# A trunk kernel's MLP: another order of the seven products, two additions fewer, and an eighth PSUM bank

## The chip, the core and the metric

The kernel runs on one core of one Trainium2 chip. The metric is the device time of one execution in microseconds (us); the time before is the median of three runs. Engines are named as in the profile: PE is TensorE, PEld its weight loads, DVE VectorE, ACT ScalarE, POOL GpSimd, SP SyncE.

## The reference, cut to what matters

One layer on a sequence of 512 rows of 1024 channels, in fp32: a token-mixing sub-layer (window attention, spatial gating, pooling, gates), cross-attention into 256 memory rows, and a squared-ReLU MLP, each between RMSNorms. The change touches the MLP, and the PSUM banks of everything before it:

```
hf = rmsnorm(x, g_norm[l, 4])
yf = jnp.square(jax.nn.relu(hf @ w_up[l])) @ w_down[l]     # w_up 1024 x 4096, w_down 4096 x 1024
x = x + rmsnorm(yf, g_norm[l, 5])
```

## The kernel before

Every fp32 factor is split into a high and a low part in the type fp32r (`split`: ACT casts the high part, DVE subtracts it from the source), and each product is three matmuls (`mm3`): high by high, high by low, low by high. PE's instructions keep their program order; the other engines' order is set by the tile framework's scheduler when the program is built. Each engine, and each DMA queue, works its own instructions in order.

The 4096 hidden rows come in 32 blocks of 128. Blocks 0 to 7 are made by plain products (`up`, step `U`). Blocks 8 to 31 are made two at a time (`two`, step `V`) by a scheme with seven half-sized products in place of eight (60 matmuls of 256 columns in the step, 24 left over for the next). The blocks are then used in four groups (`FIRST`, `NPAIR`: 4, 8, 8, 8 blocks) and a rest of four that a plain product takes at the end (`down`, step `D`). The product of a group with w_down is again done with seven products (`product`, step `M g i`, i from 1 to 7), two row tiles `tb` each. A product leaves its sum in PSUM bank y or z of its `tb`, and `ADDED` says into which quarter of the result (`acc`, tiles `c`) DVE adds that bank, and with which sign. Products 7, 6 and 4 accumulate onto the bank that product 1 began, 3 onto the one that 5 began.

The two last products of a step `V` are held back (`rest`): product 7 of the pair (`seventh`) runs between the two row tiles of the next step `M`, product 4 (`fourth`) after them. Both use one bank; DVE's `add(c22, c22, y)` has to read it between them.

The order of the steps is written out by hand. The operands of a step are prepared two steps ahead (`prepare`, called at the end of each step): `ready` splits the group's blocks (tiles `wloa`), forms sums of them (tiles `s`), and splits w_down's tiles (`wlob` from `q`). Products 1, 5, 6 and 4 all use one set of weight tiles, `qs[g, (0, 0)]`: after each of the first three has been split, `plus` adds the next quarter of w_down onto it by an accumulating DMA on POOL's queue, as the next of these products needs. `two_ready` loads and splits w_up's tiles (`wraw` into `wlou`). Their buffers, four `wraw`, are shared with the quarters (1, 0) and (1, 1) of w_down for products 2 and 3, and their DMAs stand in SP's queue in program order.

Before the MLP, PSUM has a pool of seven banks that `bank()` hands out in turn, and one bank, `t0`, that lies idle until the MLP.

Of the kernel before, what the change touches and what calls it, by code (L numbers as in the profile page):

```python
# [10 lines left out]
F32 = mybir.dt.float32  # L11
# [5 lines left out]
P = 128  # L17
# [5 lines left out]
M = 256  # L23
# [39 lines left out]
def trunk(ctx: ExitStack, tc: tile.TileContext, xT, xt0, memT, wst, cst, vec, rows, wsp, wpl, out):  # L63
# [8 lines left out]
    p1 = ctx.enter_context(tc.tile_pool(name="p1", bufs=1, space=bass.MemoryType.PSUM))  # L72
    cp = ctx.enter_context(ExitStack())
    pp = cp.enter_context(tc.tile_pool(name="pp", bufs=7, space=bass.MemoryType.PSUM))
# [7 lines left out]
    def slot(name, dt=F32, shape=None):  # L82
        return sl.tile(shape or [P, S], dt, name=name, tag="slot", bufs=NSLOT)
# [12 lines left out]
    def pair_of(pool, name):  # L96
        return tuple(pool.tile([P, S], F32R, name=name + z, tag="act", bufs=2 * KD) for z in "hl")

    def bank(name="ps"):
        return pp.tile([P, 512], F32, name=name, tag="ps")  # L100


    keep = tc.keep_in_program_order
# [46 lines left out]
    def split(hi, lo, src, order=free):  # L150
        return (order(nc.scalar.copy(hi, src)).ins,  # L151
                order(nc.vector.tensor_tensor(lo, src, hi.bitcast(F32), op=ALU.subtract)).ins)  # L152

    def split_scaled(hi, lo, src, g, order=free):
        order(nc.scalar.activation(hi, src, AF.Identity, scale=g))
        order(nc.vector.scalar_tensor_tensor(lo, src, g, hi.bitcast(F32), op0=ALU.mult, op1=ALU.subtract))
# [10 lines left out]
    def cut(act, lo, hi):  # L167
        return tuple(z[:, lo:hi] for z in act)

    def halfcut(hf):  # L170
        return hf * HALF, (hf + 1) * HALF
# [41 lines left out]
    with ExitStack() as c1:  # L213
# [9 lines left out]


        warm, ps = slot("warm"), bank()
        nc.vector.memset(warm[:, :P], 0.0)
        nc.vector.memset(ones, 1.0)
# [68 lines left out]
        def quad(name, dt=F32R):  # L296
            return a.tile([P, 4, S], dt, name=name, tag="y", bufs=4)
# [98 lines left out]
        c, u = quad("c", F32), quad("u", F32)  # L396
# [62 lines left out]
        def sub(o, p, q):  # L459
            nc.vector.tensor_tensor(o, p, q, op=ALU.subtract)  # L460

        def add(o, p, q):
            nc.vector.tensor_tensor(o, p, q, op=ALU.add)  # L463
# [4 lines left out]
        def each(y):  # L468
            return [tuple(z[:, b, :] for z in y) for b in range(4)]
# [9 lines left out]
        def quarters(j):  # L479

            lo, hi = rows2[j], rows2[2 + j]
            with tc.issue_after(exps[-1]):
                for i in range(2):
                    for r, k in ((lo, 2 * j + i), (hi, 4 + 2 * j + i)):
                        nc.scalar.activation(r[:, i, :], r[:, i, :], AF.Identity, scale=vc[:, V_G + k:V_G + k + 1])
            a0, a1, b0, b1 = lo[:, :, :HALF], lo[:, :, HALF:], hi[:, :, :HALF], hi[:, :, HALF:]

            def cast(i, src, sign=None):
                h, l = (z[:, 2 * j:2 * j + 2, :] for z in xs[i])
                if sign:  # L490
                    split_scaled(h, l, src, sign)
                else:
                    split(h, l, src)

            sub(b1, b1, a1)
            cast(5, b1)
            sub(a1, a0, a1)
            cast(7, a1)
            add(a0, a0, b1)
            cast(6, a0, -1.0)  # L500
            sub(b0, a0, b0)
            cast(3, b0)
# [132 lines left out]
        def merged(hf):  # L635
# [18 lines left out]
        steps = [("B", 0, 0), ("B", 0, 1), ("S",), ("P",)] + [("G", 0, i) for i in G] + [("G", 1, i) for i in G] + [  # L654
            ("B", 1, 0), ("B", 1, 1)] + [("G", 2, i) for i in G] + [("E", 0), ("E", 1)]
# [293 lines left out]
    with ExitStack() as c3:  # L949
        f = c3.enter_context(tc.tile_pool(name="f", bufs=1))  # L950
# [26 lines left out]
        def tiles_of(g, ab):  # L977

            n = NPAIR[g] // 2
            at = T_DN + FIRST[g] + (2 * ab[0] + ab[1]) * n  # L980
            return range(at, at + n)
# [20 lines left out]
        for j in range(UPK, UP0):  # L1002
            ps = bank()
# [7 lines left out]
        def held(name):  # L1011
            return pools.get(name, pools.get("")).tile([P, 512], F32, name=name, tag=name)

        for j in range(UP0):
            ps = held("t0") if j == UP0 - 1 else bank()
# [27 lines left out]
        def quarters():  # L1043

            def joined(hf, c, t):
                for j in range(4):
                    h, l = cut(xf[4 * c + j], *halfcut(hf))
                    add(t[:, j, :], h.bitcast(F32), l.bitcast(F32))
                return t

            def room(name, tag, bufs):
                return f.tile([P, 4, HALF], F32, name=name, tag=tag, bufs=bufs)

            def new(i):
                h, l = (f.tile([P, 4, HALF], F32R, name=f"xs{i}{z}", tag="xs", bufs=6) for z in "hl")
                xs[i] = [(h[:, j, :], l[:, j, :]) for j in range(4)]
                return h, l

            a21, a22 = joined(1, 0, room("x21", "s", 2)), joined(1, 1, room("x22", "q", 4))
            sub(a22, a22, a21)  # L1060
            a11 = joined(0, 0, room("x11", "q", 4))
            sub(a21, a11, a21)
            split(*new(7), a21)
            add(a11, a11, a22)
            split_scaled(*new(6), a11, -1.0)
            for j in range(4):
                for part in cut(xf[4 + j], *halfcut(0)):
                    sub(a11[:, j, :], a11[:, j, :], part.bitcast(F32))
            split(*new(3), a11)

            def last():
                for j in range(4):
                    split(*xs[5][j], a22[:, j, :])

            return last
# [75 lines left out]
        acc, sums = {}, {}  # L1151
# [16 lines left out]
        def ready(g, i):  # L1168

            def new(name):  # L1170
                t = f.tile([P, 4, HALF], F32, name=name, tag="s", bufs=2)
                sums[g, name] = [t[:, j:j + 2, :] for j in range(0, NPAIR[g], 2)]
                return sums[g, name]

            def each(op, *of):
                for z in zip(*of):
                    op(*z)

            def plus(ab, of):

                for q, i in zip(qs[g, ab], tiles_of(g, of)):
                    nc.gpsimd.dma_start(q, wst[i], accum_op=ALU.add)  # L1182

            a0, a1 = halves(g, 0)
            if i == 1:
                first, second = a0, (0, 0)
            if i == 7:
                first, second = new("s3"), (0, 1)
                each(sub, first, a0, a1)
            if i > 1 and i != 7:  # L1190
                b0, b1 = halves(g, 1)
            if i == 5:
                first, second = new("s1"), (0, 0)
                each(sub, first, b1, a1)
            if i == 6:
                first, second = sums[g, "s1"], (0, 0)
            if i == 4:
                first, second = b1, (0, 0)
            if i == 3:
                first, second = sums[g, "s1"], (1, 1)  # L1200
                each(sub, first, first, b0)
            if i == 2:
                first, second = b0, (1, 0)
            if i in (2, 3):
                loads(g, second)
            act, ws = parts(g, first, i), []
            if i == 5:
                each(add, first, first, a0)
            for q in qs[g, second]:
                w = parts_of(f"b{i}")  # L1210
                split(*w, q)
                ws.append(w)
            if i in (1, 5, 6):
                plus((0, 0), {1: (0, 1), 5: (1, 1), 6: (1, 0)}[i])
            return act, ws
# [1 line left out]


        BANKS = {1: "y", 7: "y", 6: "y", 4: "y", 5: "z", 3: "z", 2: "y"}
        ADDED = {1: ((0, 0, 1), (0, 1, -1)), 7: ((0, 1, 1),), 6: ((0, 1, -1), (1, 1, -1)), 4: ((1, 0, 1),),  # L1220
                 5: ((1, 1, -1),), 3: ((0, 1, -1),), 2: ((0, 0, 1),)}
        banks = {}

        def product(g, i, act, ws, between=None):
            for tb in range(2):
# [5 lines left out]
                for j in range(NPAIR[g]):  # L1231
# [3 lines left out]
                    for n, (q1, q2) in enumerate(((0, 0), (0, 1), (1, 0))):  # L1235
                        mm(ps, lhsT=w1[q1], rhs=w2[q2], start=new and j == 0 and n == 0,
                           stop=j == NPAIR[g] - 1 and n == 2, skip_group_check=not new)
                for hf, c, sign in ADDED[i]:
                    if (hf, c, tb) not in acc:
# [58 lines left out]
            return finish  # L1298


        steps = [("M", 0, 1), ("U", 5), ("M", 0, 5), ("U", 6), ("M", 0, 7), ("M", 0, 6), ("U", 7), ("M", 0, 3), ("M", 0, 4), ("M", 0, 2)]
        for g in range(1, 4):
            u = FIRST[g] + 4
            steps += [("V", u), ("M", g, 1), ("V", u + 2), ("M", g, 7), ("V", u + 4), ("M", g, 5), ("M", g, 6), ("V", u + 6),
                      ("M", g, 4), ("M", g, 3), ("M", g, 2)]
        steps += [("D",)]

        def prepare(st):
# [24 lines left out]
        for n, st in enumerate(steps):  # L1333
# [6 lines left out]
            elif st[0] == "M":  # L1340
                product(st[1], st[2], *got.pop(n), rest)
                if rest and steps[n - 1][1] >= FIRST[4]:
                    for j in range(2):
                        i = steps[n - 1][1] + j
# [85 lines left out]
```

## Time and profile before

| | |
|---|---|
| median of three runs | 794.5 us (792.24 to 796.3) |
| the profiled execution: time, span | 793.82 us, 792.1 us |
| PE busy | 777.4 us, 98% of the span |
| DVE, ACT, POOL busy | 616.0, 472.1, 65.6 us |
| granted clock of PE | 0.998 of full speed |

The times of the profile count from the span's start; the profiled execution is 1.7 us longer than its span. The MLP's first group begins near 484 us, the three equal groups run from 522 to 762 us, and `down` ends the kernel.

### The profile page before, as it was taken

Reading aid. Unit: us, or ns where it says so; the run is one execution under the profiler, and the core shown is the slowest. Engines: PE = TensorE matmul, PEld = TensorE weight load, DVE = VectorE, ACT = ScalarE, POOL = GpSimd, SP = SyncE. Lnnn points to the kernel's source line nnn. Section 1 sums busy time; section 2 is a strip of 40 time slices with the busy share of each in tenths; the row PEclk is TensorE's granted clock in tenths of the full one; section 3 lists DMA queues with packets and bytes.
Section 4 is the critical chain, followed back from the end, with each engine's and each line's share of the span. In section 5 each row is a group of like instructions: output and inputs, shape, how many; then the busy total and the mean of one; then the engine's idle time right before and its main releaser. Section 6 shows DMA issues by size and latency. Waiting matters only on the chain.

```text
span 792.1 us, 11400 instructions
## 1 busy us (share of the span) xinstructions
PE 777.4 (98%) x4250; PEld 670.6 (85%) x4250; DVE 616.0 (78%) x942; ACT 472.1 (60%) x877; POOL 65.6 (8%) x93
## 2 busy tenths in 40 slices
PE   9999999999999999999999999999999999999996
PEld 7887778878888888888888899899899989888985
DVE  6677975888758656568758759898899877998966
ACT  7327879756563463544757576667565755565732
POOL 0000000200101000251100010010100010001000
PEclk9999999999999999999999999999999999999999
DMA  6443222735756233653322454584676357546522
GB/s 231 160 141 126 80 80 64 202 78 188 167 207 138 75 107 107 228 212 122 109 102 66 173 161 107 173 217 142 115 224 167 134 107 211 155 152 122 164 81 101
DMA packets 34567, 112.79 MB, mean 142 GB/s; under 512 B 4176, under 2 KB 4688, under 8 KB 34512
## 3 DMA queue, kind: packets, MB, share of 16 engines
q1 hardware_dynamic: 27296, 86.64, 32.0%
q0 software_dynamic: 7072, 25.17, 16.1%
q8 instruction: 33, 0.54, 0.3%
q10 hardware_dynamic: 144, 0.26, 0.1%
q14 instruction: 22, 0.18, 0.1%
HBM read 107.86 MB, written 4.19 MB: 141 GB/s over the span
## 4 chain that ended last, share of the span: by engine, by line
PE 76%; DVE 8%; issue 7%; DMA 5%; ACT 3%; SPq 0%; POOL 0%; POOLq 0%; DVEq 0%; ACTq 0%
PE ps L106 48%; PE y L106 9%; PE t L106 7%; PE v L106 6%; PE z L106 3%; DMA q<-wst 3%; PE ps L109 2%; DMA wraw<-wst 2%; DVE wlo L152 1%; DVE s L331 1%; DVE mx L333 1%; ACT s L339 1%; ACT s L349 1%; ACT whi L151 1%; DVE wlou L152 1%
## 5 line engine op out<-in xcount | busy, mean ns | idle before, releaser
L152 DVE TENSOR_TENSOR wlo<-wraw,whi 128x1024 fp32r<-128x1024 f32 (+2 forms) x70 | 81.2, 1169 | 37.4 <-ACT whi L151 37.2
L151 ACT CAST whi<-wraw 128x1024 fp32r<-128x1024 f32 (+2 forms) x70 | 69.5, 1000 | 49.0 <-DMA wraw<-wst 33.7
L151 ACT CAST whiu<-wraw 128x512 fp32r<-128x512 f32 (+1 forms) x60 | 47.0, 792 | 37.2 <-DVE wraw L958 22.2
L152 DVE TENSOR_TENSOR wlou<-wraw,whiu 128x512 fp32r<-128x512 f32 (+1 forms) x60 | 53.0, 902 | 6.5 <-ACT whiu L151 6.0
L106 PE MATMUL y<-whib,whia 128*128 128x512 f32 x140 | 54.8, 391 | 0.0
L106 PE MATMUL y<-wlob,whia 128*128 128x512 f32 x140 | 54.8, 391 | 0.0
L106 PE MATMUL y<-whib,wloa 128*128 128x512 f32 x140 | 54.5, 389 | 0.0
L152 DVE TENSOR_TENSOR wlob<-q,whib 128x1024 fp32r<-128x1024 f32 x35 | 41.9, 1223 | 10.6 <-ACT whib L151 10.6
L152 DVE TENSOR_TENSOR wlog<-wq,whig 128x1024 fp32r<-128x1024 f32 x30 | 36.4, 1222 | 12.0 <-ACT whig L151 11.8
L151 ACT CAST whig<-wq 128x1024 fp32r<-128x1024 f32 x30 | 31.1, 1048 | 24.1 <-DVE acc L463 7.2
L151 ACT CAST whib<-q 128x1024 fp32r<-128x1024 f32 x35 | 35.8, 1047 | 14.4 <-DMA q<-wst 11.5
L1182 POOL DMA_DIRECT2D q<-wst x21 | 18.1, 863 | 183.6 <-DVE wlob L152 149.4
L106 PEld LDWEIGHTS y<-whib,wloa 128*128 128x128 f32 x140 | 26.3, 188 | 5.6
L106 PEld LDWEIGHTS y<-whib,whia 128*128 128x128 f32 x140 | 26.4, 188 | 4.9
L106 PEld LDWEIGHTS y<-wlob,whia 128*128 128x128 f32 x140 | 26.4, 188 | 4.6
L339 ACT ACTIVATE s<-s,ng 128x256 f32<-128x256 f32 x32 | 15.9, 499 | 14.6 <-DVE ng L335 14.5
L958 DVE TENSOR_TENSOR c<-c,y 128x512 f32<-128x512 f32 x28 | 19.1, 685 | 5.3 <-PE y L106 5.3
L106 PE MATMUL z<-whib,whia 128*128 128x512 f32 x56 | 21.9, 392 | 0.0
L106 PE MATMUL z<-wlob,whia 128*128 128x512 f32 x56 | 21.9, 391 | 0.0
L152 DVE TENSOR_TENSOR wlog<-wrawq,whig 128x1024 fp32r<-128x1024 f32 x12 | 14.7, 1224 | 9.3 <-ACT whig L151 9.3
L106 PE MATMUL z<-whib,wloa 128*128 128x512 f32 x56 | 21.8, 389 | 0.0
L151 ACT CAST whig<-wrawq 128x1024 fp32r<-128x1024 f32 x12 | 12.6, 1051 | 12.2 <-issue 8.3
(1161 smaller groups left out, 2668.4 us busy)
## 6 DMA issues: line engine op xcount, KB each, us to landing
wraw<-wst SPq DMA_DIRECT2D x88, 512.0 KB, 3.2
q<-wst POOLq DMA_DIRECT2D x28, 512.0 KB, 5.9
q<-wst SPq DMA_DIRECT2D x14, 512.0 KB, 3.7
wrawq<-wst SPq DMA_DIRECT2D x12, 512.0 KB, 3.3
wq<-wst SPq DMA_DIRECT2D x12, 512.0 KB, 4.2
wq<-wst POOLq DMA_DIRECT2D x12, 512.0 KB, 6.1
xr<-xT SPq DMA_DIRECT2D x4, 512.0 KB, 6.6
x<-xt POOLq DMA_DIRECT2D x8, 256.0 KB, 6.1
```

The source lines that it names most:

```text
L106: keep(nc.tensor.matmul(*args, **kw))
L109: keep(nc.tensor.transpose(o, i, ident))
L151: return (order(nc.scalar.copy(hi, src)).ins, order(nc.vector.tensor_tensor(lo, src, hi.bitcast(F32), op=ALU.subtract)).ins)
L152: order(nc.vector.tensor_tensor(lo, src, hi.bitcast(F32), op=ALU.subtract)).ins)
L331: nc.vector.tensor_tensor(prob[i][:, 2 * bp:2 * bp + 2, :], raws[i][bp].rearrange("p (j k) -> p j k", j=2), mask, op=ALU.add)
L333: nc.vector.tensor_reduce(mx, prob[i], op=ALU.max, axis=AX.X)
L339: nc.scalar.activation(z, z, AF.Exp, bias=ng[:, b:b + 1], scale=0.125, accum_out=den[:, b:b + 1])
L349: nc.scalar.activation(z, z, AF.Identity, scale=rd[:, b:b + 1])
L958: nc.vector.tensor_tensor(o, p, q, op=ALU.add)
L1182: nc.gpsimd.dma_start(q, wst[i], accum_op=ALU.add)
```

## The change

The order of the seven products becomes 1, 5, 6, 7, 3, 4, 2 in place of 1, 7, 5, 6, 4, 3, 2, and the last two, 4 and 2, are put into the next group, behind its first step `V` (after the last group they stand by themselves). Product 1 and product 6 are now added into one quarter each, not two, and 7 is subtracted from another quarter than it was added to: seven additions for each row tile of a group in place of nine. The sum for product 7 (`s3`) is formed with those of product 5. `bank()` takes the idle bank `t0` at each eighth call. Two tiles of 64 bytes, which nothing uses, move the MLP's sums of x in memory.

```diff
     def bank(name="ps"):
-        return pp.tile([P, 512], F32, name=name, tag="ps")
+        nbank[0] += 1
+        return (pp if nbank[0] % 8 else p1).tile([P, 512], F32, name=name, tag="ps" if nbank[0] % 8 else "t0")
...
+            def shift(i):
+                f.tile([P, 16], F32, name=f"shift{i}", tag=f"shift{i}", bufs=1)
+            shift(0)
             a21, a22 = joined(1, 0, room("x21", "s", 2)), joined(1, 1, room("x22", "q", 4))
...
             split(*new(7), a21)
+            shift(1)
...
             if i == 7:
-                first, second = new("s3"), (0, 1)
-                each(sub, first, a0, a1)
+                first, second = sums[g, "s3"], (0, 1)
...
             if i == 5:
                 each(add, first, first, a0)
+                each(sub, new("s3"), a0, a1)
...
-        ADDED = {1: ((0, 0, 1), (0, 1, -1)), 7: ((0, 1, 1),), 6: ((0, 1, -1), (1, 1, -1)), 4: ((1, 0, 1),),
+        ADDED = {1: ((0, 0, 1),), 6: ((0, 1, -1),), 7: ((1, 1, -1),), 4: ((1, 0, 1),),
                  5: ((1, 1, -1),), 3: ((0, 1, -1),), 2: ((0, 0, 1),)}
...
-        steps = [("M", 0, 1), ("U", 5), ("M", 0, 5), ("U", 6), ("M", 0, 7), ("M", 0, 6), ("U", 7), ("M", 0, 3), ("M", 0, 4), ("M", 0, 2)]
+        steps = [("M", 0, 1), ("U", 5), ("M", 0, 5), ("U", 6), ("M", 0, 6), ("U", 7), ("M", 0, 7), ("M", 0, 3)]
         for g in range(1, 4):
             u = FIRST[g] + 4
-            steps += [("V", u), ("M", g, 1), ("V", u + 2), ("M", g, 7), ("V", u + 4), ("M", g, 5), ("M", g, 6), ("V", u + 6),
-                      ("M", g, 4), ("M", g, 3), ("M", g, 2)]
+            steps += [("V", u), ("M", g - 1, 4), ("M", g - 1, 2), ("V", u + 2), ("M", g, 1), ("V", u + 4), ("M", g, 5), ("V", u + 6), ("M", g, 6), ("M", g, 7), ("M", g, 3)]
+        steps += [("M", 3, 4), ("M", 3, 2)]
```

## Rows read from the trace of the kernel before

**Rows 1.** Page, part 1: busy time and share of the span of each engine.
```profile
PE 777.4 (98%) x4250; PEld 670.6 (85%) x4250; DVE 616.0 (78%) x942; ACT 472.1 (60%) x877; POOL 65.6 (8%) x93
```

**Rows 2.** Windows: the MLP's three equal groups; length, then each engine's busy time.
```profile
521.96:600.56 78.60, 78.60 (x505) 71.76 (x504) 72.14 (x105) 51.05 (x86) 6.90 (x8) 1.00 0.63 169
600.56:680.67 80.11, 78.86 (x505) 71.75 (x504) 68.75 (x99) 47.85 (x81) 6.91 (x8) 1.00 0.59 153
680.67:762.12 81.45, 79.39 (x506) 71.73 (x505) 73.30 (x104) 52.38 (x88) 5.18 (x6) 1.00 0.54 149
```

**Rows 3.** Chain that ended last, 600 us on: start, length, what.
```profile
600.72 2.88 PE v L106 x24
...
607.92 2.75 PE y L106 x12
```

**Rows 4.** Timeline of PE at the MLP's four stalls: start, us; idle before in brackets.
```profile
647.22 0.39 PE L106 MATMUL v<-xf4h,whiu 128*128 128x256 f32 x1 [1.25 <-DVE r L958]
...
685.93 0.39 PE L106 MATMUL v<-xs6h,whiu 128*128 128x256 f32 x1 [0.78 <-ACT r L1123]
...
696.80 0.38 PE L106 MATMUL v<-xf4h,whiu 128*128 128x256 f32 x1 [0.81 <-DVE r L958]
...
728.65 0.39 PE L106 MATMUL v<-xf4h,whiu 128*128 128x256 f32 x1 [0.47 <-DVE r L958]
```

**Rows 5.** Timeline of DVE before the first of these stalls.
```profile
643.27 2.36 DVE L152 TENSOR_TENSOR wlob<-q,whib 128x1024 fp32r<-128x1024 f32 x2 [3.20 <-ACT whib L151]
...
646.75 0.41 DVE L958 TENSOR_TENSOR r<-r,v 128x256 f32<-128x256 f32 x1
```

**Rows 6.** Timeline of POOL: the first accumulating DMA ahead of that stall.
```profile
633.40 0.86 POOL L1182 DMA_DIRECT2D q<-wst  x1 [27.53 <-ACT r L1143]
```

**Rows 7.** Timeline of ACT: two casts that waited for DMAs.
```profile
642.19 1.99 ACT L151 CAST whib<-q 128x1024 fp32r<-128x1024 f32 x2 [3.17 <-DMA q<-wst]
...
670.25 1.05 ACT L151 CAST whiu<-wraw 128x1024 fp32r<-128x1024 f32 x1 [2.90 <-DMA wraw<-wst]
```

**Rows 8.** Timeline of DVE and of SP's queue around the second of those casts.
```profile
661.69 1.23 DVE L152 TENSOR_TENSOR wlob<-wrawq(1, 1)_6496,whib 128x1024 fp32r<-128x1024 f32 x1
...
671.33 1.23 DVE L152 TENSOR_TENSOR wlou<-wraw,whiu 128x1024 fp32r<-128x1024 f32 x1 [3.71 <-ACT whiu L151]
...
662.94 20.81 SPq L1081 DMA_DIRECT2D wraw<-wst  x6
```

**Rows 9.** Groups by line and form, DVE's additions of banks y and z into the result.
```profile
L958 DVE TENSOR_TENSOR c<-c,y 128x512 f32<-128x512 f32 x28 | 19.1, 685 | 5.3 <-PE y L106 5.3
L955 DVE TENSOR_TENSOR c<-c,y 128x512 f32<-128x512 f32 x22 | 14.3, 684 | 0.0
L955 DVE TENSOR_TENSOR c<-c,z 128x512 f32<-128x512 f32 x14 | 9.5, 681 | 0.1
```

**Rows 10.** Timelines of PE and DVE in product 1 of the last group.
```profile
691.65 0.28 PE L106 MATMUL v<-xs7h,whiu 128*128 128x256 f32 x1
...
694.53 0.68 DVE L958 TENSOR_TENSOR c<-c,y 128x512 f32<-128x512 f32 x1
695.13 0.68 DVE L955 TENSOR_TENSOR c<-c,y 128x512 f32<-128x512 f32 x1
...
696.33 0.42 DVE L958 TENSOR_TENSOR r<-r,v 128x256 f32<-128x256 f32 x1
```

**Rows 11.** Timelines of PE and DVE where a PSUM bank came late, before the MLP.
```profile
85.86 0.50 PE L106 MATMUL ps<-xg0h,whi 128*128 128x512 f32 x1 [0.94 <-DVE yal L152]
...
90.72 0.69 DVE L152 TENSOR_TENSOR t2l<-ps,t2h 128x512 fp32r<-128x512 f32 x1
...
159.96 0.69 DVE L619 TENSOR_TENSOR sp<-ps,bsp 128x512 f32<-128x512 f32 x1 [0.84 <-PE ps L106]
...
162.78 1.29 DVE L619 TENSOR_TENSOR sp<-ps,bsp 128x512 f32<-128x512 f32 x2
...
163.62 0.47 PE L106 MATMUL ps<-whig,xg0h 128*128 128x512 f32 x1 [0.32 <-DVE sp L619]
```

More of the change, by code (lines that the diff above doesn't have):

```diff
@@ L97, in pair_of @@
         return tuple(pool.tile([P, S], F32R, name=name + z, tag="act", bufs=2 * KD) for z in "hl")
+    nbank = [0]
     def bank(name="ps"):
-        return pp.tile([P, 512], F32, name=name, tag="ps")
+        nbank[0] += 1
+        return (pp if nbank[0] % 8 else p1).tile([P, 512], F32, name=name, tag="ps" if nbank[0] % 8 else "t0")
     keep = tc.keep_in_program_order
```

## The prediction

> **What bounds the kernel now.** The page's busy times come first: PE is busy for 777.4 us, 98% of the span [rows 1]. A change that leaves the number of matmuls alone can only win what PE stands still, and what follows its last matmul. The seven products stay seven, so I look for where PE stands still in the MLP.
>
> The windows show it best. The three groups of eight blocks do the same work: 505 or 506 matmuls and some 71.7 us of weight loads each. They take 78.60, 80.11 and 81.45 us [rows 2]. In the first PE is busy throughout, so 78.60 us is the floor for any order, and the second and third lose (80.11 − 78.60) + (81.45 − 78.60) = 1.51 + 2.85 = 4.36 us. That is all that a new order can win there. The timeline of PE says where: four matmuls waited, three for DVE's `add(c22, c22, y)` (the product `v<-xf4h` is `fourth`, held until that addition has read the bank) and one for ACT's copy of a half block (`r L1123`) [rows 4]. DVE is busy for 72.14 of 78.60 us and 73.30 of 81.45 us of a group [rows 2], so it has little room to catch up.
>
> What made DVE late is read backwards from the stalls. Before the first, DVE stood 3.20 us in front of `wlob`, the split of product 6's weights, with the wanted addition behind it in its queue [rows 5]. ACT's cast ahead of that split had waited for a DMA until 642.19 us [rows 7], the accumulating DMA that POOL issued at 633.40 us [rows 6]: 8.8 us from issue to cast. In the old order only one step `V` lies between the preparation of product 5 (whose split frees the tiles for the DMA) and that of product 6. A step `V` has 60 matmuls at 2.88/24 = 0.12 us [rows 3], 7.2 us: less than 8.8. The same pair of steps holds the fourth stall.
>
> The second and third stalls come after another DMA. ACT waited for `wraw` until 670.25 us [rows 7] and DVE behind it 3.71 us [rows 8]. That DMA could start only when product 3's split at 661.69 us had freed the buffer: SP's queue issued it at 662.94 us [rows 8]. After that loss DVE ran behind through the next step and a half. Its addition for product 1 began at 694.53 us, though PE had left the tile at 691.65 us, 2.9 us earlier; a second addition into another quarter stood between it and the one that `fourth` waited for [rows 10].
>
> **The change, part by part.** *The order: weights.* A step `M` after a `V` takes two tiles of 2.75 us [rows 3] and twice 12 held-back matmuls of 1.44 us: 8.4 us; another `M` takes 5.5 us. From product 5's preparation to product 6's there are now a `V` and an `M`, 15.6 us; from 1 to 5 as much (before 31), from 6 to 4 26.6 us (before 13.9). All exceed the 8.8 us that the DMA needs, by 6.8 us at least, which covers DVE's lateness of 2.9 us. POOL's queue gets the same DMAs; those of the next group come later, but still have V + M + M, 21 us, before product 1 needs them.
>
> *The order: raw buffers.* With product 2 moved behind the first `V`, that step's `wraw` tiles take the buffers of the previous `V`, freed before that one began, not those of product 3. The 3.71 us of DVE's idle time go. Product 2 takes those of product 3, which are split before product 3 starts, a step and a `V` (12.7 us) ahead; SP's queue has no other new wait.
>
> *The additions.* DVE adds 28 + 22 + 14 = 64 times at 0.68 us [rows 9]; seven of nine per tile leave 48 (the eight first ones are ACT's copies before and after), 16 × 0.684 = 10.9 us of DVE. PE hides them, so in themselves they are worth nothing, but where DVE is late each takes 0.60 us out of the queue (695.13 − 694.53) [rows 10]. The moved `s3` puts two such operations, 1.2 us, into product 5's preparation. Product 1's step of 8.4 us hides them.
>
> Of the 4.36 us I therefore count all as gone, and then charge what the new order brings.
>
> *The order: banks.* Products 6 and 7, and 4 and 2, now follow each other directly and use the same two banks, so PE must wait until DVE has read the first one's tile. At a lateness of 2.9 us and an addition of 0.68 us the bank is free 3.6 us after PE left it [rows 10]. The cover after a `V` is 1.44 + 2.75 + 1.44 = 5.6 us for the first tile, 4.2 us for the second: nothing. In the last group, 4 and 2 stand alone with 2.75 us, in the first they have half-sized tiles, 2.8 us for the second: up to 0.85 us at three places if DVE is late there, 2.5 us in all, none if it is not. I take 0.6 us: near the lower end, since the steps before 4 and 2 prepare only one product each.
>
> That two engines must not meet in a bank is what PE's wait of 1.25 us for `r L958` shows [rows 4]. The Trainium skill has it as a rule (PSUM — Partial Sum Buffer, section "PSUM bank collisions raise a hardware error"): accesses of different engines to one bank have to be kept apart by semaphores. Read as a wait of 0.85 us at each of the seven new pairs of neighbours, it would charge 6.0 us in place of 0.6 and bring the sum to 794.9 us; the covers just counted speak against that.
>
> *The eighth bank.* Two waits of PE before the MLP are for a bank still being read [rows 11]. At 163.62 us the first gate product waits 0.32 us for `sp L619`, the pair of reads from 162.78 us, and starts again with a slow matmul of 0.47 us: I take 0.4 us in all, an estimate. With eight banks it would take the one that was read one use earlier, from 159.96 us. From there PE works without a break; I count the 0.4 us fully. The wait before 85.86 us, 0.94 us idle, about 1.1 us with the refill, lies in the attention, where DVE sets the pace: with it gone, PE would stand before `t2l`, which DVE starts only at 90.72 us [rows 11]. Between 0 and 1.1 us I take 0.2.
>
> *The 64 bytes.* DVE's groups read quite different tiles and lie at 681 to 685 ns [rows 9]; at 4 ns an instruction no place matters. Nothing, hidden by PE; without cover under 0.4 us for a hundred of them.
>
> **The sum**, on the profiled execution's own 793.82 us (0.7 us below the median of the three): 793.82 − 4.36 − 0.4 − 0.2 + 0.6 = 789.5 us. The tail after `down` keeps its order. At the good ends of the bounds it is 793.82 − 4.36 − 0.4 − 1.1 = 788.0 us, at the bad ones 791.6 us (no gain in the attention, 2.5 us for banks).
>
> **The rivals.** *DVE stays the bound* (same): its 72 us per group fall only by four additions of 0.60, 2.4 us, to some 69 of 78.6. The waits for `add(c22, c22, y)` come back at other steps, as preparations of a `V` now stand ahead of it in products 1 and 5. Against it speaks group 1, which ran without a stall at 72.14 us of DVE. With three waits of 1 us: 793.82 − 4.36 + 3 − 0.4 − 0.2 = 791.9 us.
>
> *The attention is reordered for the worse* (same): the scheduler sees another bank and orders DVE and ACT differently where DVE sets the pace. One more wait of the present size in place of one less, 1.1 + 0.2 us: 790.8 us.
>
> *The shared bank stops PE* (slower): the next `V`'s preparation (two splits of 1.18 us [rows 5] and seven operations of 0.60 us, 6.6 us) is queued ahead of product 4's additions. The bank then comes 2.9 + 6.6 + 0.7 = 10.2 us late against a cover of 5.6, three times over: 13.8 us, 793.82 − 4.36 − 0.4 − 0.2 + 13.8 = 802.7 us. It decides once the three waits pass 5 us together, from a lateness of some 7.3 us. For it: DVE is mostly busy; against it: the step before is a `V` with a light preparation, and the additions shown were only 2.9 us late [rows 10].
>
> **How the numbers follow.** The likeliest case has 0.60 (its own range 788.0 to 791.0), the DVE rival 0.28, the attention 0.06, the bank 0.06. A change under 0.5%, 4 us, can't be told from none here; 790.5 us is the bound to faster. Most of the first case lies below it, the next two above: faster 0.57, same 0.38, slower 0.05. The range from 787.8 to 793.0 leaves out the bank rival and the ends of the others.
>
> **What would show it.** The three groups of eight in the windows at 78.6 to 79 us each; no wait of PE for `r L958`; ACT's casts of `q` and `wraw` without long waits for DMAs; 48 additions of banks; the first gate product after `wpool` without a wait. Waits of PE for `c` from y (the bank rival) or still for `r` (the DVE rival) would show it wrong.

## The result, and the profile after

The changed kernel takes 789.25 us in the median of eight runs (788.38 to 790.66), the kernel before 794.72 us in eight runs beside it. The ratio is 0.994, with a 95% interval of 0.9922 to 0.9957: a gain of 0.4 to 0.8%, small but clear of the spread. The profiled execution took 789.55 us with a span of 787.4 us, against the sum's 789.5. One execution of the first experiment below took 2760 us, its 512-column matmuls starting every 839 ns in place of 227 for a reason that is not known, and is left out of that row (with it the median is 791.21 us).

The first part of its page (busy time, share of the span, instructions) answers to [rows 1]:

```profile
PE 777.1 (99%) x4250; PEld 669.2 (85%) x4250; DVE 607.5 (77%) x926; ACT 472.0 (60%) x877; POOL 65.9 (8%) x93
```

PE's work is the same and DVE has 16 instructions fewer. The windows, as in [rows 2], begin here at the first matmul of each group's first step V:

```profile
515.67:588.69 73.02, 73.02 (x481) 66.96 (x480) 64.53 (x94) 48.63 (x84) 6.13 (x8) 1.00 0.60 153
588.69:667.05 78.36, 78.36 (x505) 71.37 (x504) 69.46 (x99) 49.48 (x84) 6.92 (x8) 1.00 0.61 162
667.05:745.65 78.60, 78.60 (x506) 71.50 (x504) 70.18 (x100) 52.78 (x90) 6.92 (x8) 1.00 0.66 171
745.65:757.22 11.57, 11.27 (x49) 8.93 (x48) 8.17 (x9) 3.97 (x4) 0.00 (x0) 1.00 0.34 116
```

The second and third window hold a group's full work of 505 matmuls: 78.36 and 78.60 us, the floor of 78.60 that the first group of before had. (The first is shorter because its products 4 and 2 are the half-sized ones of the first group; the last holds the products 4 and 2 that stand alone.) In the MLP the list of PE's waits (us in total, times, longest) has one entry, and none for `r`:

```profile
PE y L110 <- DVE c L962: 0.3, 1, 0.3
```

On the timelines this is the second row tile of the last product 2, which follows product 4 in the same bank. First PE, then DVE:

```profile
753.67 0.39 PE L110 MATMUL y<-whib,wloa 128*128 128x512 f32 x1
754.36 0.50 PE L110 MATMUL y<-whib,whia 128*128 128x512 f32 x1 [0.30 <-DVE c L962]
```

```profile
752.49 1.23 DVE L156 TENSOR_TENSOR wlo<-wraw,whi 128x1024 fp32r<-128x1024 f32 x1 [2.22 <-ACT whi L155]
753.63 0.68 DVE L962 TENSOR_TENSOR c<-c,y 128x512 f32<-128x512 f32 x1
```

From start to start 0.69 us pass in place of 0.23: 0.46 us lost. The addition stood behind the split of a tile for `down`, for which DVE had waited 2.22 us. The weights of product 6 no longer come late. POOL issues their sum at 626.60 us, and ACT casts them at 639.70 us, 13.1 us later, without a wait before it ([rows 6, 7] had 8.8 us and a wait of 3.17):

```profile
626.60 0.87 POOL L1192 DMA_DIRECT2D q<-wst  x1 [10.85 <-DVE wlob L156]
```

```profile
639.70 1.03 ACT L155 CAST whib<-q 128x1024 fp32r<-128x1024 f32 x1
```

DVE's groups by line and form count 20 + 14 + 14 = 48 additions of banks, where [rows 9] count 64:

```profile
L962 DVE TENSOR_TENSOR c<-c,y 128x512 f32<-128x512 f32 x20 | 13.6, 681 | 3.6 <-PE y L110 3.6
L959 DVE TENSOR_TENSOR c<-c,y 128x512 f32<-128x512 f32 x14 | 9.6, 684 | 4.5 <-PE y L110 4.4
L959 DVE TENSOR_TENSOR c<-c,z 128x512 f32<-128x512 f32 x14 | 9.4, 680 | 0.0
```

**Where the 4.7 us of the span went.** Up to the MLP's first group of eight blocks: before it began at 521.96 us, behind two half-sized products of 5.50 us that now stand inside it, so 516.46 us is to be compared with 515.67: 0.8 us. The eighth bank works in this stretch, but only some 0.5 us can be put down to it (see its experiment): seven traces with eight banks enter the group anywhere from 515.2 to 516.6 us. From there to `down`: 762.12 − 516.46 = 245.66 us before, 757.22 − 515.67 = 241.55 now: 4.1 us, which is the 4.36 us of the stalls less 0.46 for the new wait; the 0.2 us left over fit matmuls that run a little faster (see the 64 bytes). The end: 30.0 us before, 30.2 now.

### The profile page after: what moved, and what is told of

Its sections match the earlier page's. It is cut to its first block, busy times and chain, and to the rows that moved or that the text cites. A ratio compares the mean times of both kernels' runs of the same rounds, so it can differ in the third digit from the quotient of the medians.

```text
span 787.4 us, 11392 instructions
## 1 busy us (share of the span) xinstructions
PE 777.1 (99%) x4250; PEld 669.2 (85%) x4250; DVE 607.5 (77%) x926; ACT 472.0 (60%) x877; POOL 65.9 (8%) x93
## 4 chain that ended last, share of the span: by engine, by line
PE 87%; DVE 5%; ACT 3%; DMA 3%; issue 1%; POOL 0%; SPq 0%; POOLq 0%; DVEq 0%; ACTq 0%
PE ps L110 48%; PE y L110 12%; PE t L110 10%; PE v L110 10%; PE z L110 5%; PE ps L113 2%; DMA g<-rows 1%; DMA wraw<-wst 1%; ACT sx L870 1%; DVE wlo L156 1%; DMA x<-xT 1%; ACT s L353 1%; DVE mx L337 1%; DVE s L335 1%; ACT s L343 1%
## 5 line engine op out<-in xcount | busy, mean ns | idle before, releaser
L155 ACT CAST whia<-s 128x512 fp32r<-128x512 f32 x21 | 12.6, 619 | 12.5 <-PE t L110 11.9
```

The lines of the kernel that those rows point to most:

```text
L155: return (order(nc.scalar.copy(hi, src)).ins, order(nc.vector.tensor_tensor(lo, src, hi.bitcast(F32), op=ALU.subtract)).ins)
```

## The experiments

Each time is a median, with the range of its runs; "before" is the kernel before on the same chip, run beside it.

| what runs | median, us | range | before | ratio, 95% interval |
|---|---|---|---|---|
| after | 789.25 | 788.38 to 790.66 | 794.72 | 0.9922 to 0.9957 |
| old order, seven additions | 790.87 | 790.2 to 791.75 | 795.32 | 0.9941 to 0.9975 |
| new order, nine additions | 789.47 | 789.23 to 790.16 | 795.32 | 0.9920 to 0.9962 |
| old order, third sum of weights left out | 789.19 | 787.9 to 790.32 | 795.32 | 0.9913 to 0.9954 |
| old order, only 4 and 2 moved | 794.81 | 792.21 to 796.86 | 795.32 | 0.9980 to 1.0015 |
| after without the 64 bytes | 789.37 | 788.62 to 789.91 | 794.65 | 0.9922 to 0.9948 |
| after without the eighth bank | 790.20 | 788.79 to 790.93 | 794.65 | 0.9930 to 0.9958 |
| after, product 2 in bank z | 789.42 | 789.0 to 789.81 | 794.65 | 0.9922 to 0.9951 |
| after, all operands 64 bytes on | 789.97 | 789.5 to 790.48 | 794.65 | 0.9929 to 0.9958 |
| after, activations 64 bytes on | 794.24 | 793.28 to 794.72 | 794.73 | 0.9983 to 1.0011 |
| after, xs 192 bytes on, product 2 in z | 786.18 | 785.47 to 787.48 | 794.75 | 0.9882 to 0.9913 |
| after again, beside the row above | 789.94 | 789.36 to 790.81 | 794.75 | 0.9930 to 0.9955 |

**Was DVE late because of its additions?** The kernel before with two additions per row tile dropped:

```diff
-        ADDED = {1: ((0, 0, 1), (0, 1, -1)), 7: ((0, 1, 1),), 6: ((0, 1, -1), (1, 1, -1)), 4: ((1, 0, 1),),
+        ADDED = {1: ((0, 0, 1),), 7: ((0, 1, 1),), 6: ((1, 1, -1),), 4: ((1, 0, 1),),
```

> The kernel before with its own order and its seven banks, but with two additions per row tile left out (product 1's and product 6's into the quarter (0, 1)), so that part of the result is missing: 48 additions in place of 64, only the load of DVE is changed. Order theory (late DMAs make DVE late): DVE's wait of about 3.2 us in front of product 6's wlob and ACT's wait of about 2.9 us for wraw stay, PE still waits for r at product 5 and in the last group; at most one addition of 0.60 us goes out of each late stretch, so the time falls by 0.6 to 1.8 us, to 793 or 794. Load theory (additions make DVE late): all four stalls go, 4.4 us, and the time is 790.0 to 790.8.

790.87 us: 4.5 us below before, just above the load theory's range. The kernel ran once more for its trace:

> The same kernel as in the first run of the old order with seven additions, for its trace. That run's median was 791.2 us, between the two theories. Mixed theory (each of the two remedies is enough for most of the loss, since DVE has a few us to spare in a group): the waits for the DMA q and the DMA wraw are still there, but PE waits for r and for the copy less than 1 us in all in place of 3.3. Order theory: waits of 2 to 3.3 us stay. Load theory: the waits for the DMAs go too, because DVE frees the buffers earlier.

791.14 us, 3.6 below the kernel before that ran beside it. The timelines of ACT and of PE (idle before in brackets) come nearest to the mixed theory:

```profile
640.35 1.05 ACT L151 CAST whib<-q 128x1024 fp32r<-128x1024 f32 x1 [3.12 <-DMA q<-wst]
...
717.97 1.05 ACT L151 CAST whib<-q 128x1024 fp32r<-128x1024 f32 x1 [3.23 <-DMA q<-wst]
```

```profile
642.02 0.39 PE L106 MATMUL v<-xs7h,whiu 128*128 128x256 f32 x1 [0.76 <-ACT r L1131]
...
725.59 0.38 PE L106 MATMUL v<-xf4h,whiu 128*128 128x256 f32 x1 [0.53 <-DVE r L958]
```

The late DMAs are still there, as long as in [rows 7]. But PE lost only 0.76 and 0.53 us by them, 1.29 us in all, where the mixed theory allowed 1 us, and the two stalls in and behind the last group's first step V are gone, with the wait for `wraw`, which that theory had kept. The kernel before shows the same thing by itself: in its first group of eight, which ran without a stall, ACT waited for such a DMA too:

```profile
560.05 1.05 ACT L151 CAST whib<-q 128x1024 fp32r<-128x1024 f32 x1 [2.65 <-DMA q<-wst]
```

So here a late DMA stops PE only where DVE and ACT have no slack left for it.

**Were nine additions enough for a stall in the new order?** The kernel after with the two additions put back:

```diff
-        ADDED = {1: ((0, 0, 1),), 6: ((0, 1, -1),), 7: ((1, 1, -1),), 4: ((1, 0, 1),),
+        ADDED = {1: ((0, 0, 1), (0, 1, -1)), 6: ((0, 1, -1), (1, 1, -1)), 7: ((1, 1, -1),), 4: ((1, 0, 1),),
```

> The kernel after with the two additions per row tile put back (product 1 and product 6 are each added into a second quarter, which puts terms into the result that don't belong there): 64 additions in the new order. Order theory: no wait of PE for r, groups of 78.4 to 78.9 us, time within 0.6 us of the kernel after, 789.3 to 789.9. Load theory: DVE is late again by up to 2.4 us in a group, PE waits for r or for c, and the time is 791.5 to 794.

789.47 us, 0.2 above the kernel after, which the spread of the runs can't tell from nothing. The list of PE's waits shows one for DVE's `r`, which the order theory had not expected:

```profile
PE t L110 <- DVE r L962: 0.7, 1, 0.7
```

So the order by itself takes nearly all away, and the additions bring at most what this one wait costs.

**Which DMA?** The kernel before without the accumulating DMAs behind product 5:

```diff
-            if i in (1, 5, 6):
+            if i in (1, 6):
                 plus((0, 0), {1: (0, 1), 5: (1, 1), 6: (1, 0)}[i])
```

> The kernel before, but the accumulating DMAs behind product 5 are left out (product 6 and what follows use weights that lack one term): nothing stands between the two splits of 5 and 6 but ACT and DVE themselves. Order theory: DVE's 3.2 us in front of product 6's wlob go, and with them PE's waits for r of 1.25 and 0.47 us at product 5; the second and third stall (0.78 and 0.81 us) stay, since the wraw buffers are as before: 792.3 to 793.2. Load theory: the waits for r stay, since DVE has the same 64 additions: 794.0 to 794.8.

789.19 us, below the ranges of both theories: more was won than the order theory gave it. SP's queue, ACT and PE:

```profile
659.94 33.85 SPq L1081 DMA_DIRECT2D wraw<-wst  x8
```

```profile
667.26 1.05 ACT L151 CAST whiu<-wraw 128x1024 fp32r<-128x1024 f32 x1 [1.57 <-DMA wraw<-wst]
```

```profile
693.82 0.39 PE L106 MATMUL v<-xf4h,whiu 128*128 128x256 f32 x1 [0.51 <-DVE r L958]
```

Nothing was done to the raw buffers, and yet SP issued the `wraw` DMA at 659.94 in place of 662.94 us [rows 8], ACT waited 1.57 us in place of 2.90, and of the four stalls one of 0.51 us is left. The transfer itself was no faster: 7.3 us from issue to cast in both. The split of product 3, which frees the buffer, had been 3 us late itself, for DVE had lost 3.2 us before product 6. So about half of ACT's second wait (1.33 of 2.90 us), and 1.08 of the 1.59 us that PE lost in the second and third stall, came from the first.

**And the raw buffers alone?** The kernel before, with its order of 1, 7, 5, 6 and nine additions, but with 4 and 2 moved into the next group:

```diff
...
-            steps += [("V", u), ("M", g, 1), ("V", u + 2), ("M", g, 7), ("V", u + 4), ("M", g, 5), ("M", g, 6), ("V", u + 6),
-                      ("M", g, 4), ("M", g, 3), ("M", g, 2)]
+            steps += [("V", u), ("M", g - 1, 4), ("M", g - 1, 2), ("V", u + 2), ("M", g, 1), ("V", u + 4), ("M", g, 7), ("V", u + 6), ("M", g, 5), ("M", g, 6), ("M", g, 3)]
+        steps += [("M", 3, 4), ("M", 3, 2)]
```

> The kernel before with its nine additions, its seven banks and its order 1, 7, 5, 6, 3, 4, 2, but with 4 and 2 put behind the next group's first step V: the raw buffers are freed early, while product 5's and product 6's preparation are still one step V (7.2 us) apart. Order theory: ACT's wait of 2.9 us for wraw and the second and third stall go (about 2 us), the wait in front of product 6's wlob stays at 2.5 to 3.5 us; without a step V behind 5 it now stops PE at 6 itself or is taken up by the cover there: 791.8 to 793. Load theory: 64 additions, so PE's waits keep their sum of some 3 us wherever they fall: 793.8 to 795.

794.81 us, no change that can be measured. This lies in the load theory's range, and PE's waits keep their sum too (2.63 + 0.5 = 3.1 us), but not by the load: the old stalls shrank to 0.5 us in all, and a new one came, in the first full group, from a DMA that waited for a buffer. SP's queue, DVE and PE there:

```profile
515.44 3.86 SPq L1081 DMA_DIRECT2D wraw<-wst  x2
```

```profile
517.73 1.21 DVE L152 TENSOR_TENSOR wlob<-wrawq(1, 0)_5040,whib 128x1024 fp32r<-128x1024 f32 x1
...
525.11 0.69 DVE L958 TENSOR_TENSOR wraw<-wraw,wraw 128x512 f32<-128x512 f32 x1 [3.30 <-DMA wraw<-wst]
```

```profile
529.30 0.39 PE L106 MATMUL v<-xf4h,whiu 128*128 128x256 f32 x1 [2.63 <-DVE r L958]
```

The second of the two issues could go out only at 515.44 + 3.86 − 0.33 = 518.97 us, when DVE had split product 2's tile (517.73 + 1.21 = 518.94). It landed after DVE had stood 3.30 us, and PE lost 2.63 us. The kernel after has the same dependence at the same place. SP's queue and DVE there:

```profile
518.63 11.58 SPq L1091 DMA_DIRECT2D wraw<-wst  x3
```

```profile
517.39 1.22 DVE L156 TENSOR_TENSOR wlob<-wrawq(1, 0)_5038,whib 128x1024 fp32r<-128x1024 f32 x1
...
522.41 0.69 DVE L962 TENSOR_TENSOR wraw<-wraw,wraw 128x512 f32<-128x512 f32 x1
```

SP issued the DMA at 518.63 us, right behind the split of product 2's tile (517.39 + 1.22 = 518.61). But here the tile was there when DVE came to it 3.8 us after the issue, where the other kernel's DVE had to wait until 6.1 us after it (525.11 − 518.97). So the full new order waits for product 2's split as well and is spared the stall by an earlier landing; what made the transfer faster was not shown.

**The eighth bank.** The kernel after with seven banks:

```diff
-        return (pp if nbank[0] % 8 else p1).tile([P, 512], F32, name=name, tag="ps" if nbank[0] % 8 else "t0")
+        return pp.tile([P, 512], F32, name=name, tag="ps")
```

> The kernel after with bank() taking the pool of seven banks only. Theory (the prediction's terms, 0.4 and 0.2 us): PE waits for sp at the first gate product again, 0.3 us and a slow matmul, and for yal near 85 us, 0.9 us, while the waits for t2l and t3l that took its place go: 0.4 to 0.9 us more, 789.7 to 790.2. Rival (the eighth bank frees the attention fully): 0.4 + 1.1 = 1.5 us more, 790.7. Rival (it brings nothing): 789.2.

790.20 us, 0.95 above the kernel after; the ranges overlap, so the traces decide. PE's timeline without it, then of the kernel after:

```profile
85.28 0.50 PE L110 MATMUL ps<-xg0h,whi 128*128 128x512 f32 x1 [0.96 <-DVE yal L156]
...
161.27 1.45 PE L110 MATMUL ps<-c,wpool 128*128 128x512 f32 x3
163.04 0.47 PE L110 MATMUL ps<-whig,xg0h 128*128 128x512 f32 x1 [0.32 <-DVE sp L623]
163.34 0.39 PE L110 MATMUL ps<-wlog,xg0h 128*128 128x512 f32 x1
```

```profile
83.79 0.49 PE L110 MATMUL ps<-xg0h,whi 128*128 128x512 f32 x1
...
89.38 0.39 PE L110 MATMUL ps<-t2h,vh 128*128 128x512 f32 x1
89.91 0.50 PE L110 MATMUL ps<-t2l,vh 128*128 128x512 f32 x1
...
99.40 0.50 PE L110 MATMUL ps<-t3l,vh 128*128 128x512 f32 x1 [0.38 <-DVE t3l L156]
...
160.96 1.45 PE L110 MATMUL ps<-c,wpool 128*128 128x512 f32 x3
161.85 0.79 PE L110 MATMUL ps<-whig,xg0h 128*128 128x512 f32 x1
162.48 0.40 PE L110 MATMUL ps<-wlog,xg0h 128*128 128x512 f32 x1
```

Both waits come back with seven banks. With eight, PE stands before `t2l` and `t3l` instead (0.53 us from start to start in place of 0.23, and a wait of 0.38). At the gates the last three matmuls of `wpool` and the first of the gates take 2.07 us with seven banks (161.27 to 163.34) and 1.52 with eight (160.96 to 162.48). From the first matmul of `t0h` to the second of the gates it takes 88.6 to 89.3 us in seven traces with eight banks (mean 89.0) and 89.1 to 89.9 us in five with seven (mean 89.5): some 0.5 us by the means, though single traces overlap.

**The 64 bytes.** The kernel after without `shift(0)` and `shift(1)`:

> The kernel after without its two tiles of 64 bytes, so that the moving operands xs of the steps V begin where they did in the kernel before. The prediction's view (the place costs or gives nothing): same spacing of matmuls as in the kernel after, same time, 789.0 to 789.5. Address theory (the trace of after shows the 432 matmuls that move xs every 117.5 ns in place of 120): the spacing is 120 ns again, 432 x 2.5 ns = 1.1 us more in the steps V; the products with w_down, which stood 2 ns further apart in the kernel after (some 580 of them, 1.0 us), may be back at 229 ns too. So 789.2 to 790.4.

789.37 us, no difference. The chain shows what hides in it (start, length, what): 24 matmuls of `xs` in a step V, then a row tile of product 1 (12 matmuls of 512 columns). After, then without the 64 bytes:

```profile
593.17 2.83 PE v L110 x24
596.00 2.76 PE y L110 x12
...
600.17 2.77 PE y L110 x12
```

```profile
593.57 2.88 PE v L110 x24
596.45 2.75 PE y L110 x12
...
600.63 2.75 PE y L110 x12
```

With the 64 bytes the `xs` matmuls are faster and the products with w_down slower. Over all starts from 520 us on: 432 of `xs` at 117.6 in place of 119.8 ns, 0.95 us won; 350 that move `whib` at 230.2 in place of 228.2, 176 that move `wlob` at 228.7 in place of 229.1, and 84 of `down` some 3 ns slower, 0.7 − 0.1 + 0.3 = 0.9 us lost.

Whose place counts? The tiles' addresses in the built program say that before, each moving operand differs from the weights loaded beside it by a multiple of 256 bytes ("beside it" are the weights of the next matmul, loaded while this one runs). In the kernel after `xs` differs by 64 or 192, and the weight tiles behind the second 64 bytes differ from the rest by 128. The next kernel puts 64 bytes below all operands, so that `xs` is back at a multiple of 128 and the others are not:

```diff
     wp = ctx.enter_context(tc.tile_pool(name="wp", bufs=1))
+    wp.tile([P, 16], F32, name="base", tag="base", bufs=1)
```

> The kernel after with a further tile of 64 bytes below all tiles that matmuls read: weights, x and factors begin 64 bytes past a multiple of 128, and the xs tiles (which the change put there) at a multiple of 128 again. Absolute theory (a moving operand that begins 64 bytes past a multiple of 128 streams faster): the xs matmuls are back at 120 ns, the 576 others of the steps V at 117.5, and the 512-column matmuls may fall below 226.7 ns: up to 2 ns x 2470 = 5 us less, 784 to 789. Relative theory (it matters whether the moving tile and the weights that are loaded beside it lie 64 bytes apart): xs at 117.5 ns and all others unchanged, since all move together: 789.2. Rival (only the place of xs among the buffers of DVE and ACT matters): xs at 117.5 ns, too, but no order in the rest: 789 to 790.

```profile
593.54 2.83 PE v L111 x24
596.37 2.76 PE y L111 x12
```

789.97 us, and the chain is that of the kernel after: the absolute theory, which had `xs` back at 120 ns, is out, and the difference of the two places is left. Then the activations of the whole kernel, 64 bytes from the weights (a tile of 64 bytes each in `sl`, `late` and `m`, as above in `wp`):

> The kernel after with a tile of 64 bytes ahead of the activations' pools (sl, late, m), so that activations begin 64 bytes past the weights' places throughout: in nearly all matmuls before the MLP and in all of the steps U, V and D the moving tile and the weights that are loaded beside it differ by 64 or 192 bytes in 256; only the products with w_down keep 0 or 128. Relative theory (from the runs with xs alone: 119.8 ns at 0, 117.8 at 64, 115.5 at 192, for 256 columns): xf matmuls at 115 to 118 ns, 1.5 to 3 us less in all, and if 512 columns gain the same 2 to 4 ns, 1800 of them give 4 to 7 us more: 779 to 786. Rival (512 columns don't gain): 787 to 788. Rival (they lose, as they do at 128, 232.2 ns against 227.4): 9 us more, 798.

794.24 us: the rival that 512 columns lose was right in kind, though it had said 798. The chain over the gates, which PE works without a break, there and in the kernel after:

```profile
179.81 35.23 PE ps L111 x151
```

```profile
179.88 35.13 PE ps L110 x155
```

35.23/151 = 233.3 ns against 35.13/155 = 226.6 ns. Grouped by the difference of the addresses (moving tile minus the weights loaded beside it, in 256 bytes), the mean from start to start in ns, with the number of matmuls:

| difference | 256 columns, steps V | 512 columns |
|---|---|---|
| 0 | 119.7 (516, after) | 227.1 (1676, after, ahead of the MLP) |
| 64 | 117.8 (396, after) | 229.4 (447, activations shifted) |
| 128 | 119.3 (60, after) | 232.2 (153, after, MLP) |
| 192 | 115.5 (36, after); 116.9 (421, activations shifted) | 233.3 (1141, activations shifted) |

In nearly all of these matmuls the weights that they work with lie at the same difference as those loaded beside them, so which of the two counts was not shown.

**Product 2 in the other banks.** One word of the kernel after:

```diff
-                 ... 5: "z", 3: "z", 2: "y"}
+                 ... 5: "z", 3: "z", 2: "z"}
```

> The kernel after with product 2 in the banks z, which product 3 has left a step and more before, in place of the banks y that product 4 has just filled: one word is changed. Theory: PE's wait of 0.46 us for c between 4 and 2 of the last group goes, and the one in the other groups, if any: 0.4 to 0.5 us less than the kernel after, 788.8. Rival: DVE, which must add 4 before 2, is the one that is late, and the wait moves to the step down behind it: 789.2.

PE no longer waits for `c`, but 789.42 us is not below the kernel after: the 0.4 to 0.5 us did not come. In a further trace of the kernel after that wait is absent too; it doesn't come in every execution.

**Both together.** Product 2 in z, and 192 bytes in place of the first 64:

```diff
-                f.tile([P, 16], F32, name=f"shift{i}", tag=f"shift{i}", bufs=1)
+                f.tile([P, (48, 16)[i]], F32, name=f"shift{i}", tag=f"shift{i}", bufs=1)
```

> The kernel after with two edits that the runs point to: product 2 in the banks z (the 0.46 us before 2 of the last group), and the first of the two 64-byte tiles made 192 bytes, so that xs differs from the weights by 192 bytes in 256 and the weight tiles behind it lie at a multiple of 256 from the others again. Relative theory: the some 200 matmuls of 512 columns at a difference of 128 fall from 232.2 to 228 ns (0.8 us), the 430 of xs stay at 117.8 ns or fall to 116.9 (0.4 us); with the 0.46 us in all 1.2 to 1.7 us less than the kernel after in the same call, 787.5 to 788.1. Rival (the place explains nothing): 0.0 to 0.5 us less.

> The kernel after, unchanged, on the same chip as the version with both edits: 789.25 us, between 788.4 and 790.7.

786.18 us against 789.94 us: the two intervals in the table don't meet, and the gain is larger than expected. Product 2 in z alone had brought nothing that can be measured, so the gain is put down to the places; they were not run alone. In the chain:

```profile
592.04 2.74 PE v L110 x24
594.78 2.73 PE y L110 x12
...
598.93 2.72 PE y L110 x12
```

All 432 of `xs` now differ by 192 bytes and start every 115.3 ns (117.6 in the kernel after): 1.0 us. The matmuls of 512 columns from 500 us on, nearly all of them products with w_down and `down`, are back at a difference of 0 and at 227.2 ns on average (229.5): 682 x 2.3 = 1.5 us. The other 0.8 us of the 3.3 between the two spans (787.3 and 784.0) lie ahead of the first group of eight blocks, where two traces of the kernel after differ by 0.4 us (515.67 and 516.11): they are not explained.

## Why the prediction was right, and where not

*The windows' floor* held: all 4.36 us are gone. That 789.5 stands against a median of 789.25 is closer than was earned. The sum forecast a fall of 4.3 us from one execution of 793.82, which lay 0.9 us below the median of the eight, 794.72. Between the two profiled executions the fall was 4.27 us, between the medians 5.5. And 78.60 us was no floor "for any order", since places of operands count too: the second window takes 78.36 us in the kernel after and 77.80 in the last version above.

*The causes of the stalls* failed in one step: "The second and third stalls come after another DMA." They were counted as a second cause, to be cured by the raw buffers. The run without the third sum shows that two thirds of these two stalls were the first DMA's lateness handed on by DVE's split: with only the first cause taken away one stall of 0.51 us stays. The buffers alone were worth nothing, and brought a wait for product 2's split that the step on raw buffers had excluded ("SP's queue has no other new wait"). The wait of SP's queue is in the full new order too, and that it cost PE nothing there was not foreseen.

*The lead of product 6's weights*, forecast at 15.6 us, came out at 13.1 from issue to cast, more than the 8.8 that had been too few.

*The additions*, "in themselves worth nothing", are worth 0.2 us or nothing in the new order, but some 4 us in the old one. What I missed is that after a late DMA DVE has to catch up, and two additions less per tile let it do so before the next step is hurt; this is how I read the traces, in which the late DMAs stay and the stalls shrink. The first group of before, which I took as evidence against the DVE rival, had a late DMA as well and no stall. Order and load are two cures of the same illness, each nearly enough; their gains don't add.

*The banks*: 0.46 us at the last 4 and 2, one of the three places named; 0.6 was taken. DVE was late there by `down`'s weights, not by another product. Read as a wait at each of the seven pairs, the rule of the Trainium skill (PSUM — Partial Sum Buffer, section "PSUM bank collisions raise a hardware error") had led to 794.9 us; the trace shows one wait, and a second trace none. Engines are kept apart in a bank, but here this costs only where the reader is late.

*The eighth bank*: 0.6 us forecast, some 0.5 by the traces. The gates gave 0.55 us in place of 0.4, and the attention about nothing in place of 0.2: there PE stands before `t2l` instead, as forecast.

*The 64 bytes*: "Nothing" is right as a sum and wrong as a reason. I looked at DVE's instructions; PE's were changed, by 0.95 us for the better and 0.9 for the worse.

## What to carry to other kernels

Where an in-order engine with little slack loses time to one late transfer, look for later waits that are only its echo before counting them as causes: take the first away and see which stay. Two remedies for one lateness must not be summed. And where PE never stops, measure the spacing of its matmuls by operand pair: the places of the operands are worth as much as a stall.

## What was not expected of the hardware

PE's pace depends on the places of its two operands to each other: with 256 columns 119.7 ns from matmul to matmul at a difference of 0, 115.3 to 116.9 at 192; with 512 columns 227.1 at 0 and 233.3 at 192, so the best place for one is the worst for the other. What in the memory does this was not shown. The Trainium skill (SBUF — State Buffer, section "Who interferes with whom") calls PE's reads of the moving operand and of the weights independent. The 233.3 against 226.6 ns of the gates, with only the activations moved, speak against that, in these matmuls at least. Nor is the difference to the next weights the whole rule: at a difference of 0 the 512-column matmuls of the MLP took 227.9 ns before, 228.7 after and 227.2 in the last version.
